# Output powers of S5 batches 5 and 6 made on VectorE ahead of the scan, batch 7 on GpSimd at another place

## The chip, the cores and the metric

The kernel runs on one core of a Trainium2 chip. The metric is the device time of one execution in microseconds (us), lower is better. The engines are TensorE (PE in the profile), its weight load (PEld), VectorE (DVE), ScalarE (ACT), GpSimd (POOL) and the queue of SyncE (SP), which issues most DMAs; ScalarE issues some too (ACTq).

## The reference

Two layers of one trunk, D_MODEL 1024, 256 context and 256 latent tokens. Layer 0 mixes tokens with a bidirectional diagonal state-space layer (S5) and a GLU, layer 1 with a gated DeltaNet; each layer ends with a squared-ReLU MLP. The change lies in S5:

```python
def _s5_direction(u, a_bar, b_bar, c_mat, h0, reverse, need_out):
    bu = jnp.einsum('blgh,gph->lbgp', u.astype(jnp.complex64), b_bar)
    ...
    a = jnp.broadcast_to(a_bar, (bu.shape[0], 1) + a_bar.shape)
    _, h = lax.associative_scan(_linear_recurrence, (a, bu), axis=0)
    final = h[-1]
    ...
    y = jnp.einsum('lbgp,ghp->blgh', h, c_mat).real
```

There are 64 groups of 16 channels with 64 complex states each; the context is scanned first, the latent tokens start from its final state.

## The kernel before, in words

The S5 phase (`s5_phase`) cuts the 64 groups into eight batches of eight, and time into chunks of eight tokens. For each batch b:

- `s5_w` (the W stage): VectorE multiplies powers of the state matrix, which TensorE has spread into a PSUM bank (`ebx`), with the input matrices (`bcB`, loaded by SP). `mul_bc` issues three operations for each half of a direction: a product to a temporary (`wtmp`, in the PSUM bank "scan"), a product to W, and their sum; that is 12 operations of 128x512 a batch.
- `s5_in`: TensorE turns W (`sint`), ScalarE copies it (`Sin`), TensorE multiplies with the input (`xin`), and ScalarE copies the result to X, the per-chunk inputs of the scan.
- `s5_v`: the same products for the output side. The powers are spread into PSUM (`ecx`), copied by ScalarE to `ec`, and multiplied with the output matrices `bcC` (two buffers; `s5_vload` loads the next batch's inside `s5_v`). All eight V are made on GpSimd, in six operations of 128x1024. `s5_v` also lets ScalarE make C0 (C in the rows) from bcC.
- `s5_a8` puts the power for one chunk into the bank "scan". `s5_scan` then walks over the chunks on VectorE: 31 steps for the first half (context), 32 for the second. A step is two `scanm` products and two sums into X (X_83 in the order's rows is the context's half, X_84 the latent's).
- `s5_k`, for pairs p of batches (0 to 3): TensorE makes a strip per batch from V, W and C0, ScalarE copies it and issues four DMAs of it to DRAM (`kd`), SP reads it back in eight DMAs as the Toeplitz tile `Kt` (two buffers), TensorE multiplies (`yl`) and ScalarE copies to `yT`.
- `s5_out(b, 0)` after the first half: ScalarE copies states (`Hs`), TensorE multiplies with V (`yp`), ScalarE applies GELU (`yg`), VectorE turns it (`yT`). `s5_out(b, 1)` does so for the second half. The GLU (weights split into `whi` and `wlo`) and the MLP follow, then the second layer.

No order is written out. Each piece is a `Task` with a priority and the tasks that it comes after; `drive` always takes the next step of the task that a modelled clock lets start first, and records its instructions in that order with their priorities. So a change of one task can move others, and the second layer is planned with a clock whose start is set against that of the first. The early pool (`ce`, with lam, sel, pw and the W tiles) is closed once the W stage and a8 are planned, and the late pool takes its memory, tile by tile, each writer waiting for the readers of what lay there. Nearly all instructions are recorded by one helper, so the profile has them under L268, and they are told apart by tile names.

Of the kernel before, what the change touches and what calls it, by code (L numbers as in the profile page):

```python
# [8 lines left out]
F32 = mybir.dt.float32  # L9
# [306 lines left out]
def drive(clock, tasks, grain=0.25, until=None):  # L316

    live = [t for t in tasks if t.end is None]
    while live and not (until and all(t.end is not None for t in until)):
        best = None  # L320
        for t in live:
            if any(d.end is None for d in t.after) or t.held or (t.gate and t.gate.free == 0):
                continue
            start = max([t.ready] + [d.end for d in t.after])
            start = clock.probe(t.eng, start)[0] if clock.fill and t.eng != "sync" else max(start, clock.t.get(t.eng, 0.0))
            key = (int(start / grain), t.prio)
            if best is None or key < best[0]:
                best = (key, t)
        assert best, "no step can go on"
        t = best[1]  # L330
        clock.step = 0.0
        clock.prio = t.prio
        try:
            r = next(t.gen)
            t.gate = r if isinstance(r, Slots) else None
            t.held = r is HOLD
            if r is HOLD:
                continue
            for o in live:
                o.held = False  # L340
            if not t.gate:
                t.ready = clock.step if r is None else r
        except StopIteration:
            t.end = t.ready = max(t.ready, clock.step)
            live.remove(t)
            for o in live:
                o.held = False
    clock.prio = None
    clock.base = clock.tc.cur_priority = clock.base + 400000
    return live  # L350
# [98 lines left out]
class K:  # L449
# [63 lines left out]
    def ada(self, l, b, pool):  # L513

        nc = self.nc
        acc = self.bank(f"ada{l}{b}", "ada", bufs=1)
        bias = pool.tile([128, 512], F32, name="adab", bufs=1)
        for kt in range(8):
            if kt == 0:
                nc.sync.dma_start(bias, self.I["ada_b"][l, b])  # L520
            while len(self.aw.get((l, b), ())) < 2 * kt + 2:
                yield HOLD
            ws = self.aw[l, b][2 * kt:2 * kt + 2]
            yield ws[1][2]
            for q in range(4):
                nc.tensor.matmul(acc[32 * q:32 * q + 32, :], self.crep[:, kt].rearrange("p a b -> p (a b)"),
                                 ws[q // 2][0][:, q % 2 * 512:q % 2 * 512 + 512], start=kt == 0, stop=False, skip_group_check=True)
            if kt == 6:
                nc.tensor.matmul(acc, self.ident, bias, start=False, stop=False, skip_group_check=True)
            for _, ring, _ in ws:  # L530
                if ring:
                    ring.give()
            yield
        row = pool.tile([128, 512], F32, name="arow", tag="adab", bufs=1)
        nc.scalar.copy(row, acc)
        if b:
            self.arow[l, b] = self.dram.tile([128, 512], F32, name=f"arow{l}{b}")
            nc.sync.dma_start(self.arow[l, b], row)
        yield
        tp = self.bank(f"adat{l}{b}", "aux", bufs=self.naux) if self.naux else self.bank(f"adat{l}{b}")  # L540
        for q in range(4):
            nc.tensor.transpose(tp[:, q * 128:q * 128 + 128], row[:, q * 128:q * 128 + 128], self.ident)
        src = tp.rearrange("p (q v j s r) -> p v j q s r", q=4, v=2, j=2, s=2)
        for v in range(2):
            dst = self.mcol[l][:, 2 * b + v].rearrange("p s (j q) -> p j q s", j=2)
            nc.scalar.copy(dst, src[:, v, :, :, :, 0])
        yield
# [240 lines left out]
    def s5_v(self, b, Vv, eng, late):  # L788

        nc = self.nc  # L790
        yield from self.Cslots.take()
        bc = self.bcC[b]
        ec = self.ec[b]
        self.Vt[b] = Vv
        C0 = self.C0[b] = late.tile([128, 2, 8, 16], F32, name="C0", bufs=NC0)
        nc.scalar.activation(C0, bc[:, 0], AF.Identity, scale=self.nsg)
        for d in range(2):
            dve = eng is nc.vector
            tmp = late.tile([128, 8, 4 if dve else 8, 16], F32, name="vtmp" + "d" * dve, bufs=1)
            self.mul_bc(eng, Vv[:, d], tmp, ec[:, :, :, d], bc[:, :, d], d == 1)  # L800
            if d == 0 and b < 7:
                self.s5_vload(b + 1, late)
            yield

    def s5_k(self, p, late):
# [449 lines left out]
def s5_phase(ctx, k):  # L1255

    nc = k.nc
    with ExitStack() as cs:
# [5 lines left out]
        V57 = [k.long.tile([128, 2, 8, 8, 16], F32, name=f"V{b}") for b in (5, 6)]  # L1264
# [5 lines left out]
        k.nsg = mid.tile([128, 1], F32, name="nsg")  # L1270

        def ecs(b):
            p = k.bank("ecx")[:, 0:256]
            k.expand(p.rearrange("p (k l d g) -> p k l d g", k=2, l=8, d=2), k.pw, b, (2, 3))
            k.ec[b] = mid.tile([128, 2, 8, 2, 8], F32, name="ec", bufs=3)
            nc.scalar.copy(k.ec[b].rearrange("p a b c d -> p (a b c d)"), p)

            yield

        def vgen(b):  # L1280
            Vv = V57[b - 5] if b in (5, 6) else (k.long if b < NV else k.late).tile([128, 2, 8, 8, 16], F32, name=f"V{b}")
            yield from k.s5_v(b, Vv, nc.vector if b in VD else nc.gpsimd, mid)

        def seq(*gens):
            for g in gens:
                yield from g

        T = Task
        VD = ()
        NV = 7  # L1290
        we, ws, ins, V, Kk, outs = [], [], [], {}, {}, []
        k.early = E = k.pool(ce, "early", 1)
# [24 lines left out]
        lds = T(seq(ld, *(k.ada_load(l, b) for l, b in more)), 0, [], "sync")  # L1317
        a0 = T(k.ada(0, 0, mid), 0, [], "tensor")
        a1 = T(seq(*(k.ada(l, b, mid) for l, b in more)), 9, [a0], "tensor")
        xn = T(xg, 1, [], "vector")  # L1320
        u = T(k.s5_u(mid), 2, [a0, xn], "vector")
        for b in range(8):
            we.append(T(k.s5_we(b), 2, we[-1:], "tensor"))
            ws.append(T(k.s5_w(b), 3, ws[-1:] + we[-1:], "vector"))
            ins.append(T(k.s5_in(b), 4, [ws[b], u] + ins[-2:-1], "tensor"))
        a8 = T(k.s5_a8(), 3, [ws[-1]], "vector")
        Ec = []
        for b in range(8):
            Ec.append(T(ecs(b), 1, Ec[-1:] + [V.get(b - 3)], "tensor"))
            if b >= NV:  # L1330
                break
            V[b] = T(vgen(b), 5, [V.get(b - 1 - (b - 1 in VD)), Ec[b]], "gpsimd")
        k.Kslots = Slots(0)
        for p in range(NV // 2):
            Kk[p] = T(k.s5_k(p, mid), 5, [V[2 * p + 1], u, ws[2 * p + 1]], "tensor")
        rest = drive(k.clock, [lds, a0, a1, xn, u, a8] + we + ws + ins + Ec + list(V.values()) + list(Kk.values()), until=ins + Ec + [a8])
        ce.close()
        k.late = k.pool(cs, "late", 1, reuse_waits="tile")
        k.yT = k.late.tile([128, 8, 512], F32, name="yT")
        k.ktp = k.pool(ck, "kt", 1, side="right", reuse_waits="tile")  # L1340
        k.Kslots.free = NKT
        scan = [T(k.s5_scan(0, 31), 0, [], "vector"), T(k.s5_scan(31, 63), 0, [], "vector")]
        scan[0].after += ins
        scan[1].after = [scan[0]]
        for b in range(NV, 8):
            V[b] = T(vgen(b), 5, [V.get(b - 1 if b not in VD and b - 1 not in VD else b - 2), Ec[b]] if b not in VD else [Ec[b]], "vector" if b in VD else "gpsimd")
        for p in range(NV // 2, 4):
            Kk[p] = T(k.s5_k(p, mid), 2, [V[2 * p + 1]], "tensor")
        for b in range(8):
            outs.append(T(k.s5_out(b, 0), 1, [Kk[b // 2], scan[0]] + outs[-1:], "tensor"))  # L1350

        rest = drive(k.clock, rest + scan + [V[b] for b in range(NV, 8)] + [Kk[p] for p in range(NV // 2, 4)] + outs,
                     until=outs + [a1, lds])
# [16 lines left out]
        rest = drive(k.clock, rest + outs + ys[0] + ys[1] + [glu, ld, sp], until=ys[1] + [glu])  # L1370
# [745 lines left out]
def tile_backbone(ctx, tc, *args):  # L2116
# [5 lines left out]
    k.wraw = k.pool(ctx, "wraw", 4, side="right")  # L2122
    c0 = ctx.enter_context(ExitStack())
    xr, cg, rest = s5_phase(c0, k)
    k.stream = Stream(k, nc.vector)
    cp = ctx.enter_context(ExitStack())
# [90 lines left out]
```

## Time and profile before

| | |
|---|---|
| timed runs | 1636.46 us median of 3 (1634.3 to 1636.75) |
| profiled execution | 1630.61 us, span 1628.8 us |
| mean granted clock of TensorE | 0.951 |
| busy: PE, DVE, ACT, POOL | 1467.9, 1105.0, 777.4, 654.3 us |

The span is the stretch of the trace from the first to the last instruction; the profiled execution's own time is 1.81 us more. Busy shares are averages over stages with different limits. In the rows, "[14.74 <-ACT X]" says that the engine stood idle for 14.74 us ahead of this instruction and that ScalarE's write of X ended the wait. A row with x4 has four instructions of one kind in a run.

### The profile page before, as it was taken

The page shows a single profiled execution, that of the slowest core. Times are in us where ns is not written, and L with a number is a line of the kernel's source. Part 1 is how long each engine was busy: PE and PEld are TensorE (multiplying, and loading weights), DVE is VectorE, ACT ScalarE, POOL GpSimd, SP SyncE. Part 2 cuts the span into 40 slices and gives each one's busy share as a digit, 9 for nine tenths or more (in the row PEclk, how much of TensorE's full clock was granted, in tenths as well). Part 3 has the DMA queues.
Part 4 walks back from the last instruction along what each step waited for, and adds up shares of the span by engine and source line. Part 5 has one row for each costly group of instructions (what it writes and reads, how often), then busy time and mean ns, then how long its engine had stood idle before and what let it go on. Part 6 is the DMA issues. An engine that isn't in the chain of part 4 may idle for free.

```text
span 1628.8 us, 31232 instructions
## 1 busy us (share of the span) xinstructions
PE 1467.9 (90%) x12370; PEld 1115.7 (68%) x12370; DVE 1105.0 (68%) x2011; ACT 777.4 (48%) x1637; POOL 654.3 (40%) x510
## 2 busy tenths in 40 slices
PE   6895678989999999997968898989999999989998
PEld 2454456767777777786756676767766665689997
DVE  6977798763343343347998878687869765667666
ACT  3352646543222232216456655656565755554443
POOL 3977033622333233334766543343615400014432
PEclk7997889999999999998989999999998999989999
DMA  9786623463544545331222211111211111536552
GB/s 279 264 290 91 137 98 118 156 211 113 172 147 170 188 158 181 139 106 65 79 77 67 66 54 47 53 47 50 70 39 59 44 57 61 188 127 196 182 192 91
DMA packets 76771, 200.77 MB, mean 123 GB/s; under 512 B 8784, under 2 KB 29008, under 8 KB 76368
## 3 DMA queue, kind: packets, MB, share of 16 engines
q1 hardware_dynamic: 76112, 197.78, 37.1%
q10 hardware_dynamic: 512, 0.98, 0.4%
q8 instruction: 97, 1.59, 0.4%
q14 instruction: 50, 0.41, 0.1%
HBM read 192.71 MB, written 6.03 MB: 122 GB/s over the span
## 4 chain that ended last, share of the span: by engine, by line
PE 62%; DVE 20%; ACT 6%; issue 5%; POOL 4%; DMA 3%; SPq 0%; POOLq 0%; DVEq 0%; ACTq 0%
PE w L268 32%; PE proj L268 8%; PE c L268 6%; DVE cacc L268 3%; PE ada L268 3%; DVE X L268 3%; PE wo L268 2%; POOL wlo L268 2%; DVE wlo L268 1%; DVE U L268 1%; DVE scanm L268 1%; DVE gt L268 1%; PE op L268 1%; PE qs L268 1%; DMA wraw<-in_w_dram 1%
## 5 line engine op out<-in xcount | busy, mean ns | idle before, releaser
L268 ACT CAST whi<-wraw 128x1024 fp32r<-128x1024 f32 x221 | 225.6, 1045 | 259.7 <-PE w L268 140.0
L268 POOL TENSOR_TENSOR wlo<-wraw,whi 128x512 fp32r<-128x512 f32 x129 | 181.7, 1427 | 258.4 <-ACT whi L268 233.6
L268 DVE TENSOR_TENSOR wlo<-wraw,whi 128x1024 fp32r<-128x1024 f32 (+1 forms) x189 | 222.0, 1202 | 79.9 <-ACT whi L268 79.3
L268 PE MATMUL w<-hh,whi 128*128 128x256 f32 (+1 forms) x512 | 170.5, 336 | 0.0
L268 PE MATMUL w<-hl,whi 128*128 128x256 f32 (+1 forms) x512 | 168.9, 331 | 0.0
L268 PE MATMUL w<-hh,wlo 128*128 128x256 f32 (+1 forms) x512 | 168.5, 331 | 0.0
L268 POOL TENSOR_TENSOR sq<-rl 128x512 f32<-128x512 f32 (+1 forms) x64 | 62.5, 977 | 217.1 <-ACT rl L268 213.3
L268 PE MATMUL w<-whi,h1h 128*128 128x512 f32 x384 | 148.8, 395 | 0.0
L268 PE MATMUL w<-whi,h1l 128*128 128x512 f32 x384 | 148.5, 390 | 0.0
L268 PE MATMUL w<-wlo,h1h 128*128 128x512 f32 x384 | 148.4, 389 | 0.0
L268 PE MATMUL proj<-hh,whi 128*128 128x256 f32 (+1 forms) x360 | 130.6, 363 | 10.3 <-ACT pp L268 8.4
L268 DVE TENSOR_TENSOR ma<-w,g 128x512 f32<-128x512 f32 x96 | 65.3, 687 | 103.5 <-PE w L268 103.4
L268 PE MATMUL proj<-hh,wlo 128*128 128x256 f32 (+1 forms) x360 | 125.5, 349 | 1.7 <-POOL wlo L268 1.7
L268 PE MATMUL proj<-hl,whi 128*128 128x256 f32 (+1 forms) x360 | 126.9, 352 | 0.0
L268 DVE SCALAR_TENSOR_TENSOR cacc<-pp,cw,cacc 128x520 f32<-128x520 f32 (+1 forms) x128 | 115.3, 903 | 11.5 <-ACT cacc L268 9.9
L268 POOL TENSOR_TENSOR xr<-xr,ma 128x512 f32<-128x512 f32 x56 | 81.3, 1455 | 95.9 <-DVE ma L268 95.9
L268 PEld LDWEIGHTS w<-hh,whi 128*128 128x128 f32 x512 | 98.0, 192 | 18.1 <-DVE wlo L268 4.2
L268 DVE TENSOR_TENSOR h1l<-sq,h1h 128x512 fp32r<-128x512 f32 (+1 forms) x64 | 35.5, 555 | 106.4 <-POOL sq L268 104.0
L268 PEld LDWEIGHTS w<-hl,whi 128*128 128x128 f32 x512 | 98.2, 192 | 10.5 <-issue 1.9
L268 PEld LDWEIGHTS w<-hh,wlo 128*128 128x128 f32 x512 | 97.9, 192 | 9.8 <-issue 0.8
L268 ACT ACTIVATE v<-c,vsc 64x128 f32<-64x128 f32 x224 | 80.6, 362 | 50.0 <-PE c L268 42.6
L268 POOL TENSOR_TENSOR rstd<-ms,mhalf 128x1 f32<-128x1 f32 (+2 forms) x22 | 17.3, 788 | 191.1 <-DVE ms L268 191.1
(312 smaller groups left out, 3532.2 us busy)
## 6 DMA issues: line engine op xcount, KB each, us to landing
wraw<-in_w_dram SPq DMA_DIRECT2D x128, 512.0 KB, 4.3
adaw<-in_ada_w_dram SPq DMA_DIRECT2D x92, 512.0 KB, 4.8
wraw<-in_w_in_dram SPq DMA_DIRECT2D x48, 512.0 KB, 3.2
wraw<-in_w_glu_dram SPq DMA_DIRECT2D x32, 512.0 KB, 3.3
wraw<-in_w_out_dram SPq DMA_DIRECT2D x16, 512.0 KB, 3.2
Kt<-kd SPq DMA_DIRECT2D x32, 128.0 KB, 4.9
X<-grd SPq DMA_DIRECT2D x32, 128.0 KB, 3.0
V<-in_ada_w_dram SPq DMA_DIRECT2D x4, 512.0 KB, 5.9
```

What stands on the lines that cost most here:

```text
L268: r = f(*args, **kw)
```

## The change

`VD` names the batches whose V is made on VectorE; it was empty and is now 5 and 6. Their powers stay in PSUM (`ecx` in the "hold" banks), their temporary (`vtmpd`) lies in the "scan" bank, and their output matrices come into a tile of their own, `bcCd`, with one buffer, loaded by SP inside `s5_v`. These tasks come after the last W task, and a8 comes after V[6]. V of batch 7 stays on GpSimd, comes after V[4], and is now the first tile of the late pool. The load of the ada bias (`adab`) gets the highest priority.

```diff
@@ ada
             if kt == 0:
+                prio, self.clock.prio = self.clock.prio, None if self.clock.prio is None else 0
                 nc.sync.dma_start(bias, self.I["ada_b"][l, b])
+                self.clock.prio = prio
@@ s5_v
+        dve = eng is nc.vector
         yield from self.Cslots.take()
+        if dve:
+            self.bcC[b] = self.early.tile([128, 2, 2, 8, 16], F32, name="bcCd", bufs=1)
+            nc.sync.dma_start(self.bcC[b], self.I["bc"][b, 1])
...
         for d in range(2):
-            dve = eng is nc.vector
-            tmp = late.tile([128, 8, 4 if dve else 8, 16], F32, name="vtmp" + "d" * dve, bufs=1)
+            tmp = (self.bank("vtmpd", "scan", bufs=1).rearrange("p (g t c) -> p g t c", g=8, t=4) if dve else
+                   late.tile([128, 8, 8, 16], F32, name="vtmp", bufs=1))
             self.mul_bc(eng, Vv[:, d], tmp, ec[:, :, :, d], bc[:, :, d], d == 1)
-            if d == 0 and b < 7:
-                self.s5_vload(b + 1, late)
+            if d == 0 and b < 7 and not dve:
+                self.s5_vload({4: 7}.get(b, b + 1), late)
+            if d and dve:
+                self.Hslots.give()
@@ s5_phase
         def ecs(b):
+            if b in VD:
+                yield from k.Hslots.take()
+                p = k.ec[b] = k.bank("ecx", "hold", bufs=2)[:, 0:256].rearrange("p (k l d g) -> p k l d g", k=2, l=8, d=2)
+                k.expand(p, k.pw, b, (2, 3))
+                yield
+                return
...
-        VD = ()
+        VD = (5, 6)
...
-        a8 = T(k.s5_a8(), 3, [ws[-1]], "vector")
...
-            V[b] = T(vgen(b), 5, [V.get(b - 1 - (b - 1 in VD)), Ec[b]], "gpsimd")
+            V[b] = T(vgen(b), 5, [V.get(b - 1), Ec[b]], "vector" if b in VD else "gpsimd")
+        a8 = T(k.s5_a8(), 3, [V[6]], "vector")
...
         k.late = k.pool(cs, "late", 1, reuse_waits="tile")
+        k.V7 = k.late.tile([128, 2, 8, 8, 16], F32, name="V7")
...
-            V[b] = T(vgen(b), 5, [V.get(b - 1 if b not in VD and b - 1 not in VD else b - 2), Ec[b]] if b not in VD else [Ec[b]], "vector" if b in VD else "gpsimd")
+            V[b] = T(vgen(b), 1, [V[4], Ec[b]], "gpsimd")
```

On VectorE, at the end of the W stage, the order now reads as follows (V_80 is batch 5's V, V_81 batch 6's; each group of three stands four times for a batch).

```order
L268 TENSOR_TENSOR W<-W,wtmp 128x8x64
L268 TENSOR_TENSOR vtmpd<-ecx,bcCd 128x512
L268 TENSOR_TENSOR V_80<-ecx,bcCd 128x8x64
L268 TENSOR_TENSOR V_80<-V_80,vtmpd 128x8x64
...
L268 TENSOR_TENSOR V_81<-V_81,vtmpd 128x8x64
L268 COPY scan<-pw 128x64 x2
L268 TENSOR_SCALAR scan<-pw 128x64
L268 COPY scan<-pw 128x64
```

Before, the first COPY of a8 followed on the W row; 24 operations have come between. On GpSimd, the end of V reads so in the kernel before (V_1361 is batch 7's):

```order
L268 TENSOR_TENSOR V_736<-V_736,vtmp 128x1024
L268 TENSOR_TENSOR V_81<-ec,bcC 128x1024 x2
...
L268 TENSOR_TENSOR V_1361<-ec,bcC 128x1024 x2
...
L268 TENSOR_TENSOR V_1361<-V_1361,vtmp 128x1024
L268 TENSOR_TENSOR wlo<-wraw,whi 128x512 x6
```

and so with the change (V_749 is batch 4's, V_1373 batch 7's):

```order
L268 TENSOR_TENSOR V_749<-V_749,vtmp 128x1024
L268 TENSOR_TENSOR vtmp<-ec,bcC 128x1024
L268 TENSOR_TENSOR V_1373<-ec,bcC 128x1024 x2
L268 TENSOR_TENSOR V_1373<-V_1373,vtmp 128x1024
L268 TENSOR_TENSOR vtmp<-ec,bcC 128x1024
L268 TENSOR_TENSOR V_1373<-V_1373,vtmp 128x1024
L268 TENSOR_TENSOR wlo<-wraw,whi 128x512 x6
```

The rows of batches 5 and 6 are gone, and five operations of batch 7 stand behind its first vtmp. On ScalarE, the stretch from the second pair's strips to the first yg reads so before (kd_1678 is pair 2's, kd_1832 pair 3's):

```order
L268 DMA kd_1507<-strip 16x960 x4
L268 COPY strip<-strip 128x480 x2
L268 DMA kd_1678<-strip 16x960 x3
L268 COPY yT<-yl 128x512
L268 DMA kd_1678<-strip 16x960
L268 COPY strip<-strip 128x480
L268 COPY yT<-yl 128x512
L268 COPY strip<-strip 128x480
L268 DMA kd_1832<-strip 16x960 x4
L268 COPY yT<-yl 128x512 x4
L268 COPY Hs<-X_83 64x2x128 x8
```

and so with the change (kd_1664 is pair 3's, kd_1860 pair 2's):

```order
L268 DMA kd_1664<-strip 16x960 x4
L268 COPY yT<-yl 128x512 x2
L268 COPY strip<-strip 128x480
L268 COPY yT<-yl 128x512 x2
L268 COPY strip<-strip 128x480
L268 DMA kd_1860<-strip 16x960 x2
L268 COPY yT<-yl 128x512
L268 DMA kd_1860<-strip 16x960 x2
L268 COPY yT<-yl 128x512
L268 COPY mcol_97<-adat_1849 128x8x2 x2
L268 COPY arow<-ada_1865 128x512
L268 COPY Hs<-X_83 64x2x128 x8
```

Pair 3 now comes ahead of pair 2; the yT copy between the kd issues of pair 2 is that of batch 6, and the copy arow has come ahead of Hs.

## Rows read from the trace of the kernel before

**Rows 1.** The page: its first line, and a line of its DMA issues (KB each, median us to landing).

```profile
span 1628.8 us, 31232 instructions
...
bcC<-in_bc_dram SPq DMA_DIRECT2D x8, 256.0 KB, 5.1
```

**Rows 2.** Stretches: busy us of each engine (instructions), PEclk, DMA share, GB/s.

```profile
115.00:180.00 65.00, 37.27 (x1036) 31.33 (x1032) 47.96 (x130) 18.35 (x40) 34.34 (x16) 0.77 0.71 115
...
371.00:600.00 229.00, 229.00 (x1084) 175.43 (x1084) 86.50 (x96) 68.45 (x92) 74.88 (x56) 1.00 0.46 157
...
775.00:1450.00 675.00, 613.80 (x6426) 452.38 (x6427) 521.92 (x1069) 398.57 (x1009) 264.92 (x214) 0.95 0.20 67
```

**Rows 3.** The chain that ended last, 80 to 330: start us, us, what.

```profile
127.24 2.54 DMA bcC<-in_bc_dram
...
149.77 2.42 DVE X L268
181.35 0.65 ACT Hs L268
```

**Rows 4.** Timeline of VectorE: start us, us, engine, operation, tiles [idle before <-releaser].

```profile
98.11 0.70 DVE L268 TENSOR_TENSOR wtmp<-ebx,bcB 128x512 f32<-128x512 f32 x1 [1.54 <-DMA bcB<-in_bc_dram]
...
114.52 0.49 DVE L268 COPY scan<-pw 128x64 f32<-128x64 f32 x2
...
115.31 0.23 DVE L268 COPY scan<-pw 128x64 f32<-128x64 f32 x1
...
130.86 3.30 DVE L268 TENSOR_TENSOR X<-X,scanm 128x128 f32<-128x128 f32 x2 [14.74 <-ACT X L268]
...
148.08 4.10 DVE L268 TENSOR_TENSOR X<-X,scanm 128x128 f32<-128x128 f32 x2
...
152.62 0.61 DVE L268 TENSOR_TENSOR X<-X,scanm 128x128 f32<-128x128 f32 x2
...
230.36 0.68 DVE L268 TENSOR_TENSOR wlo<-wraw,whi 128x512 fp32r<-128x512 f32 x1
```

**Rows 5.** Timeline of GpSimd, 116 to 152.

```profile
122.70 2.40 POOL L268 TENSOR_TENSOR V<-V,vtmp 128x1024 f32<-128x1024 f32 x1
...
129.95 4.07 POOL L268 TENSOR_TENSOR V<-ec,bcC 128x1024 f32<-128x1024 f32 x2 [0.29 <-DMA bcC<-in_bc_dram]
...
149.67 2.36 POOL L268 TENSOR_TENSOR V<-V,vtmp 128x1024 f32<-128x1024 f32 x1
```

**Rows 6.** Timeline of ScalarE and its DMA queue (ACTq), 126 to 194.

```profile
129.81 0.51 ACT L268 ACTIVATE C<-bcC,nsg 128x256 f32<-128x256 f32 x1 [2.53 <-DMA bcC<-in_bc_dram]
...
131.70 3.13 ACTq L268 DMA_DIRECT2D kd<-strip  x4
...
163.53 2.60 ACTq L268 DMA_DIRECT2D kd<-strip  x4
...
179.42 5.20 ACT L268 COPY Hs<-X 64x256 f32<-64x256 f32 x8 [5.20 <-DVE X L268]
...
186.69 0.38 ACT L268 ACTIVATE yg<-yp 128x256 f32<-128x256 f32 x1
...
193.24 0.59 ACT L268 COPY arow<-ada 128x512 f32<-128x512 f32 x1
```

**Rows 7.** Timeline of SP's DMA queue, three windows of it.

```profile
136.62 17.95 SPq L268 DMA_DIRECT2D Kt<-kd  x16
...
158.22 6.23 SPq L268 DMA_DIRECT2D Kt<-kd  x8
...
170.18 5.45 SPq L268 DMA_DIRECT2D Kt<-kd  x8
```

**Rows 8.** Timeline of TensorE, 160 to 235.

```profile
169.75 3.85 PE L268 MATMUL yl<-Kt,U 128*32 128x128 f32 x64 [4.15 <-DMA kd<-strip]
...
181.35 2.36 PE L268 MATMUL yl<-Kt,U 128*32 128x128 f32 x40 [6.92 <-ACT Hs L268]
...
231.10 0.80 PE L268 MATMUL glu<-wlo,yh 128*128 128x512 f32 x1 [8.20 <-DVE wlo L268]
```

More of the change, by code (lines that the diff above doesn't have):

```diff
@@ L1280, in vgen @@
         def vgen(b):
-            Vv = V57[b - 5] if b in (5, 6) else (k.long if b < NV else k.late).tile([128, 2, 8, 8, 16], F32, name=f"V{b}")
+            Vv = V57[b - 5] if b in (5, 6) else k.V7 if b == 7 else k.long.tile([128, 2, 8, 8, 16], F32, name=f"V{b}")
             yield from k.s5_v(b, Vv, nc.vector if b in VD else nc.gpsimd, mid)
@@ L1325, in s5_phase @@
             ins.append(T(k.s5_in(b), 4, [ws[b], u] + ins[-2:-1], "tensor"))
-        a8 = T(k.s5_a8(), 3, [ws[-1]], "vector")
         Ec = []
         for b in range(8):
-            Ec.append(T(ecs(b), 1, Ec[-1:] + [V.get(b - 3)], "tensor"))
+            Ec.append(T(ecs(b), 1, Ec[-1:] + [ws[-1] if b in VD else V.get(b - 3 if b < 7 else 4)], "tensor"))
             if b >= NV:
                 break
-            V[b] = T(vgen(b), 5, [V.get(b - 1 - (b - 1 in VD)), Ec[b]], "gpsimd")
+            V[b] = T(vgen(b), 5, [V.get(b - 1), Ec[b]], "vector" if b in VD else "gpsimd")
+        a8 = T(k.s5_a8(), 3, [V[6]], "vector")
         k.Kslots = Slots(0)
@@ L1335, in s5_phase @@
             Kk[p] = T(k.s5_k(p, mid), 5, [V[2 * p + 1], u, ws[2 * p + 1]], "tensor")
-        rest = drive(k.clock, [lds, a0, a1, xn, u, a8] + we + ws + ins + Ec + list(V.values()) + list(Kk.values()), until=ins + Ec + [a8])
+        rest = drive(k.clock, [lds, a0, a1, xn, u, a8] + we + ws + ins + Ec + list(V.values()) + list(Kk.values()), until=ins + Ec + [a8, V[5], V[6]])
         ce.close()
         k.late = k.pool(cs, "late", 1, reuse_waits="tile")
+        k.V7 = k.late.tile([128, 2, 8, 8, 16], F32, name="V7")
         k.yT = k.late.tile([128, 8, 512], F32, name="yT")
```

## The prediction

> **What bounds the kernel now.** I began with the page: the profiled execution has a span of 1628.8 us [rows 1], and its own time is 1630.61, 1.81 more. The three timed runs have their median at 1636.46, so 5.85 us are added when a sum made against the profile is compared with runs. The stretches come next [rows 2]. From 371 to 600 TensorE is busy for the whole 229 us, so whatever reaches that stretch earlier or later shifts the end by as much. From 115 to 180, where the change lies, TensorE is busy for 37.27 of 65 us: something else sets the pace. The chain that ended last [rows 3] says what: the load of bcC at 127.24, then VectorE's X, which is the scan, until 152, then ScalarE's copies Hs.
>
> The timeline of VectorE [rows 4] shows the same from the inside. The 24 operations of the W stage for batches 6 and 7 fill 98.11 to 114.5, so 8.2 us a batch; the first had waited 1.54 for bcB. The four a8 operations end at 115.54. Then VectorE stands still for 14.74 until the last X copy, which ScalarE held behind a C0 activation that waited 2.53 for bcC [rows 6]. That bcC was issued only when GpSimd gave its buffer free [rows 3]. From 130.86 two X operations take 3.3 to 4.1 us as long as GpSimd works, and 0.61 after it stops at 152.03 [rows 4, 5]. Five of the 31 steps of the first half are done at 152.2 and the other 26 at 179.42, where the Hs copies start [rows 6]: 1.047 us a step. After that ScalarE makes the outputs, the first yg at 186.69, and on VectorE the wlo that TensorE waits 8.20 for stands behind scan steps [rows 4, 8].
>
> One more chain runs beside this. A pair's strip goes to DRAM (kd) and comes back as Kt, and TensorE's yl needs all eight Kt transfers. From a pair's first Kt issue to its yl pass 11.5 us (158.22 to 169.75) and 11.2 (170.18 to 181.35) [rows 7, 8]. From the end of the last kd issue to the first Kt pass 1.8 (134.83 to 136.62) and 4.05 (166.13 to 170.18) [rows 6, 7]. The yl of 181.35 feeds a yT copy that stands ahead of the first yg: 5.3 us from yl to yg.
>
> **The change, part by part.** *V5 and V6 on VectorE.* Each is 12 operations of 128x512 of the W stage's three kinds with a tmp in PSUM; the trace has no such row for V, the W rows are the nearest, so 8.2 us each. I take the 1.54 wait as gone, since that bcB now stands ahead of adaw loads that it had stood behind (bounds 0 and 1.54). The W stage then ends at 113.0 and V5 at 121.2. The bcCd of batch 6 has one buffer, is issued when V5's last multiply is done (about 120.5), and needs 2.54 [rows 3] to 5.1 (the median of the eight bcC loads) [rows 1]; with 2.54 V6 waits 1.9, with 5.1 it waits 4.4. I take 2.54, the row that stood alone on the queues, as this one will. V6 ends at 131.3, a8 at 132.3. The X copies of batch 7 no longer stand behind a bcC wait and are done by then, so the old 14.74 has been filled with work: the scan starts 1.4 later than before.
>
> *V5 and V6 off GpSimd, V7 at its new place.* Twelve operations go. V7's first vtmp can run early, but its first write lies in memory that a8 reads, so five operations (2.0, 2.0, 2.4, 2.0, 2.4 by [rows 5]) run from 132.3 to 143.1 under the scan. Each holds one X operation, as the rows of 130.86 to 152 show, so two and a half steps are done at 143.1 and the other 28.5 take 29.8: the first half ends at 172.9 instead of 179.42, 6.5 earlier.
>
> Here a rule is weighed. The rows say that the X pair pays 4.10 and GpSimd nothing: its V<-V,vtmp is 2.40 ahead of the scan and 2.36 under it [rows 4, 5]. The Trainium skill ("SBUF — State Buffer", section "Who interferes with whom") states that a VectorE operation with two SBUF inputs and a GpSimd operation that reads SBUF exclude each other for a whole instruction, whoever started first. By that rule V7's operations would wait for X operations too, some 0.3 us each (half of 0.61), V7 would end 1.5 later and so would all that hangs on it, 1638.4 in place of the forecast's 1636.9; by the rows it is nothing, and the sum goes by the rows.
>
> *The K chain in its new order: pairs 0, 1, 3, 2.* V7's strip (40 small matmuls and a copy) I bound by the pace of yl, 64 in 3.85, at 2.4 us; kd of pair 3 starts at 145.5, its four issues take 2.6 [rows 6], to 148.1, and with 4.05 the first Kt is issued at 152.2. It used to be pair 2's at 158.22. Its yl comes 11.2 later, at 163.4. Now the order costs something: on ScalarE the last two kd of pair 2 stand behind the yT copy of batch 6, which needs that yl (half of 3.85, and 0.6 for the copy): 165.9. Two issues of 0.65 bring 167.2, the way to the first Kt is 1.8 to 4.05 (I take the middle, 2.9, since only two transfers are left to land), so pair 2's first Kt is issued at 170.1 and its yl starts at 181.3. Before, the last yl started at 181.35. In the old order kd of the last pair lay beside the Kt of the pair ahead; in the new one it lies behind it, and what GpSimd's earlier end gave is spent there. The first yg stays at 186.7.
>
> *The rest.* The copy arow of 0.59 moves from between yg operations [rows 6] to ahead of the Hs copies, where ScalarE has time: 0.6 gained. On VectorE one more scan step stands ahead of the wlo that TensorE waits for at 231.10 [rows 8], since the transposes moved further ahead in the scan than that wlo did: 1.05 lost. The adab issue and one wraw issue change place on SP's queue beside work that lasts longer: nothing, and at most their own half microsecond.
>
> *Sum:* 0.0 from the last yl, -0.6, +1.05: +0.4 us, so 1631.0 for the profiled execution and 1636.9 on the scale of the median. Its own range goes by the bounds of kd's way: 1.8 takes 1.1 away and 4.05 adds 1.2, so 1635.8 to 1638.1 with the other waits as taken.
>
> **The rivals.** *The scan's gain arrives.* If the kd transfers are not late, since queues are emptier and V7's strip is quick, the 6.5 us of the scan reach the outputs: -6.5 - 0.6 + 1.05 = -6.0, so 1630.5. For it speaks that the chain that ended last names DVE X and not Kt at 150 [rows 3]; against it that the last yl started after the scan's half had ended already before (181.35 against 179.42).
>
> *The K chain comes late* (the other side). V6's bcCd takes 5.1 instead of 2.54 (+2.5), the wait for bcB stays (+1.5), and kd's way is 4.05 (+1.2): all hang on one line from V6 over V7 to pair 2's Kt, so they add up: +5.2 - 0.6 + 1.05 = +5.7, 1642.2. It decides from the point where pair 2's first Kt is issued after 173.0 (170.1 + 2.9): then the loss is over 3.3. For it speaks that three of four links have a row with the longer time; against it that those rows were taken with other transfers in flight.
>
> *The later phase is planned anew.* The planner starts the second layer from a clock that moved, and between 800 and 1440 neighbours change place on all engines. TensorE is idle there for 675.00 - 613.80 = 61.2 us [rows 2]. An estimate of a tenth of it either way is 6.1 us: 1630.8 or 1643.0. Nothing in the trace says which sign.
>
> *It does nothing* falls together with the forecast, as the sum shows.
>
> **How the numbers follow.** About 0.2% (3.3 us) is what a measurement of this kernel can tell from no change. I give the forecast 0.42 (of it 0.07 faster, 0.30 same, 0.05 slower, for smaller amounts of the other cases), the scan's gain 0.19 (0.17 faster, 0.02 same), the late K chain 0.20 (0.17 slower, 0.03 same), the new plan 0.19 (0.08, 0.03, 0.08). That makes 0.32 faster, 0.38 same, 0.30 slower. The predicted time is the forecast's, 1636.9. The range takes in the scan's gain with 1.5 us to spare and reaches past both slower cases: 1629 to 1643.5.
>
> **What would show it.** In the profile after: 24 operations vtmpd and V on VectorE of 0.7 each from about 113, with a wait for bcCd of about 2 in the middle; a8's end near 132 and no wait of X behind it; X pairs of about 4 until 143 and 0.61 after; the Hs copies free to start near 173; the first Kt of the last pair near 170 and its yl near 181, with ScalarE idle in between; the first yg near 186.7. If yg comes before 184, the kd and Kt times were taken too long, and the forecast fails to the fast side; if the last Kt is issued after 173, to the slow side. If the outputs are where I put them and the time still differs by more than 3 us, the second layer's new order did it, and the stretch 775 to 1450 shows it in TensorE's idle time.

## The result, and the profile after

| | before | after |
|---|---|---|
| median of the runs, us | 1635.38 (1634.15 to 1636.75, 4 runs) | 1659.42 (1657.06 to 1663.16, 4 runs) |
| profiled execution: span, us | 1628.8 | 1661.4 |
| profiled execution: its own time, us | 1630.61 | 1663.16 |
| first yg copy on ScalarE | 186.69 | 194.16 |
| a VectorE wlo in the middle of the first layer's MLP | 428.69 | 438.21 |
| a VectorE wlo near the end of the second layer | 1554.05 | 1586.60 |

The ratio is 1.0149, with a 95% interval of [1.0127, 1.0171]: 24 us slower, against a forecast of 1636.9 and a range that ended at 1643.5. Each of the last three rows of the table is the start of one and the same instruction in the two traces. They show two losses: 7.5 us at the first yg and 9.5 by the first layer's MLP, and another 23 between the MLP and the end of the second layer (1148.39 from one wlo to the other, where it had been 1125.36). The profiled execution of before is 5 us below the median of its runs and that of after 4 above its own. On the scale of the medians the second loss is 24.0 - 9.5 = 14.5 us.

The stretches of the changed kernel, to be read beside [rows 2] (busy us of PE, PEld, DVE, ACT and POOL with their instruction counts, granted clock, DMA share, GB/s):

```profile
115.00:180.00 65.00, 34.37 (x976) 27.05 (x976) 55.26 (x157) 14.13 (x31) 10.75 (x5) 0.79 0.66 124
...
371.00:600.00 229.00, 229.00 (x1070) 172.91 (x1068) 85.73 (x96) 64.54 (x88) 74.07 (x55) 0.99 0.47 159
...
775.00:1450.00 675.00, 607.71 (x6356) 444.51 (x6355) 513.24 (x1040) 390.89 (x990) 264.16 (x213) 0.94 0.19 62
```

GpSimd does what the change says, 34.34 us of work down to 10.75 in the first stretch, and VectorE takes it over. The MLP is TensorE alone, as before, and hands on whatever delay reaches it. From 775 to 1450, in the second layer, TensorE stands idle for 675.00 - 607.71 = 67.3 us instead of 61.2, at a granted clock of 0.94 and 0.95 (mostly the upper of its two levels). These two windows do not hold the same instructions. From one wlo of the table to the other they do, first before, then after:

```profile
428.69:1554.05 1125.36, 1051.78 (x8712) 810.49 (x8713) 745.96 (x1336) 556.58 (x1246) 427.75 (x346) 0.97 0.31 103
438.21:1586.60 1148.39, 1066.12 (x8712) 819.78 (x8713) 750.00 (x1336) 558.72 (x1246) 426.03 (x346) 0.95 0.31 101
```

Of the 23.0 us, 8.7 are idle time of TensorE (82.3 instead of 73.6). In the other 14.3 it is busy longer with the same 8712 instructions, at a granted clock of 0.95 instead of 0.97.

VectorE's timeline of the changed kernel, beside [rows 4]:

```profile
120.35 0.69 DVE L268 TENSOR_TENSOR V<-V,vtmpd 128x512 f32<-128x512 f32 x1
127.91 0.70 DVE L268 TENSOR_TENSOR vtmpd<-ecx,bcCd 128x512 f32<-128x512 f32 x1 [6.87 <-DMA bcCd<-in_bc_dram]
...
136.09 0.49 DVE L268 COPY scan<-pw 128x64 f32<-128x64 f32 x2
...
137.60 3.84 DVE L268 TENSOR_TENSOR X<-X,scanm 128x128 f32<-128x128 f32 x2
...
141.87 4.00 DVE L268 TENSOR_TENSOR X<-X,scanm 128x128 f32<-128x128 f32 x2
...
146.31 2.31 DVE L268 TENSOR_TENSOR X<-X,scanm 128x128 f32<-128x128 f32 x2
...
149.05 0.61 DVE L268 TENSOR_TENSOR X<-X,scanm 128x128 f32<-128x128 f32 x2
...
194.58 0.45 DVE L268 STREAM_TRANSPOSE yT<-yg 128x256 f32<-128x256 f32 x1 [12.39 <-ACT yg L268]
```

The same transpose in the kernel before:

```profile
187.11 0.45 DVE L268 STREAM_TRANSPOSE yT<-yg 128x256 f32<-128x256 f32 x1 [2.81 <-ACT yg L268]
```

V5 ends at 121.04 (120.35 + 0.69). V6 then waits 6.87 for its matrices. The scan starts at 137.20 and is slow until GpSimd's V7 ends, then runs at the old pace. From three steps done at 148.65 and 28 more of 1.047 its first half ends at 178.0, 1.4 earlier than before. The scan is not late. The loss shows in the wait of 12.39 us at 194.58, where it had been 2.81: VectorE stands at a transpose that waits for ScalarE's first yg, and the scan's second half stands behind it.

SP's DMA queue shows why V6 waited:

```profile
105.46 12.37 SPq L268 DMA_DIRECT2D adaw<-in_ada_w_dram  x8
121.52 0.80 SPq L268 DMA_DIRECT2D wraw<-in_w_glu_dram  x2
122.38 0.42 SPq L268 DMA_DIRECT2D bcCd<-in_bc_dram  x1
...
162.71 3.50 SPq L268 DMA_DIRECT2D Kt<-kd  x5
176.88 0.34 SPq L268 DMA_DIRECT2D adab<-in_ada_b_dram  x1
177.40 5.10 SPq L268 DMA_DIRECT2D Kt<-kd  x8
```

and in the kernel before:

```profile
175.74 0.54 SPq L268 DMA_DIRECT2D adab<-in_ada_b_dram  x1
```

The buffer for batch 6's bcCd was free at about 120.3, but two wraw loads stood ahead of the load and could themselves be issued only at 121.52. It went at 122.38 and V6 started 5.5 later. At the other end pair 2's Kt (the x8) began at 177.40. The bias load adab stood ahead of it, but SP still waited 0.2 us for kd behind adab, so adab cost it nothing here.

ScalarE and its DMA queue, beside [rows 6]:

```profile
151.21 2.37 ACTq L268 DMA_DIRECT2D kd<-strip  x4
...
159.92 0.56 ACT L268 COPY strip<-strip 128x480 f32<-128x480 f32 x1 [5.16 <-DMA kd<-strip]
...
163.43 2.09 ACTq L268 DMA_DIRECT2D kd<-strip  x2
174.35 0.58 ACT L268 COPY yT<-yl 128x512 f32<-128x512 f32 x1 [11.57 <-PE yl L268]
174.36 0.78 ACTq L268 DMA_DIRECT2D kd<-strip  x2
...
184.03 0.59 ACT L268 COPY arow<-ada 128x512 f32<-128x512 f32 x1 [6.89 <-PE ada L268]
184.51 5.07 ACT L268 COPY Hs<-X 64x256 f32<-64x256 f32 x8
191.24 0.59 ACT L268 COPY yT<-yl 128x512 f32<-128x512 f32 x1 [1.66 <-PE yl L268]
...
194.16 0.38 ACT L268 ACTIVATE yg<-yp 128x256 f32<-128x256 f32 x1 [1.04 <-PE yp L268]
```

Pair 3's kd goes at 151.21, pair 2's first half at 163.43, and its second half waits 11 us more behind a yT copy that needs pair 3's products. Then arow, which stands ahead of the eight Hs copies, waits 6.89 for TensorE. The Hs copies start at 184.51, though the scan's first half has been done since 178. TensorE's rows, beside [rows 8], close the ring:

```profile
148.20 0.60 PE L268 MATMUL strip<-V,W 128*32 128x112 f32 x8 [9.63 <-POOL V L268]
...
172.15 3.86 PE L268 MATMUL yl<-Kt,U 128*32 128x128 f32 x64 [9.70 <-DMA Kt<-kd]
...
175.94 0.90 PE L268 MATMUL adat<-consts,arow 128*128 128x128 f32 x3
...
180.17 2.02 PE L268 MATMUL ada<-adab,consts 128*128 128x512 f32 x2 [3.32 <-DMA adab<-in_ada_b_dram]
...
189.25 2.79 PE L268 MATMUL yl<-Kt,U 128*32 128x128 f32 x48 [5.32 <-ACT Hs L268]
```

The ada product that arow waits for had to wait 3.32 for adab. SP issued adab at 176.88, after 8.2 us of waiting for TensorE's adat (arow and adab share one buffer), and adat stands behind pair 3's yl. In the kernel before adab went at 175.74, hardly earlier; what is new is that the Hs copies stand behind arow. So the chain is: V6 late, V7 late, pair 3's strip late, its yl at 172.15, the second half of pair 2's kd, its Kt, and beside it adat, adab, ada, arow, Hs and yg.

### The profile page after: what moved, and what is told of

Read it like the earlier page. It is cut to its first block, busy times and chain, and to the rows that moved or that the text cites. A ratio compares the mean times of both kernels' runs of the same rounds, so it can differ in the third digit from the quotient of the medians.

```text
span 1661.4 us, 31225 instructions
## 1 busy us (share of the span) xinstructions
PE 1482.7 (89%) x12370; PEld 1126.0 (68%) x12370; DVE 1114.8 (67%) x2035; ACT 779.8 (47%) x1635; POOL 631.2 (38%) x498
## 4 chain that ended last, share of the span: by engine, by line
PE 63%; DVE 16%; ACT 6%; DMA 6%; issue 5%; POOL 4%; SPq 1%; ACTq 0%; POOLq 0%; DVEq 0%
PE w L268 31%; PE proj L268 8%; PE c L268 7%; DVE cacc L268 3%; PE ada L268 3%; PE wo L268 2%; DVE vc L268 2%; POOL V L268 1%; DVE wlo L268 1%; DMA adaw<-in_ada_w_dram 1%; DVE gt L268 1%; PE qs L268 1%; ACT Hs L268 1%; PE op L268 1%; DVE X L268 1%
## 5 line engine op out<-in xcount | busy, mean ns | idle before, releaser
L268 PE MATMUL proj<-hh,whi 128*128 128x256 f32 (+1 forms) x360 | 134.8, 374 | 11.0 <-ACT pp L268 10.7
L268 DVE SCALAR_TENSOR_TENSOR cacc<-pp,cw,cacc 128x520 f32<-128x520 f32 (+1 forms) x128 | 111.4, 872 | 13.6 <-ACT cacc L268 12.3
```

The source lines that it names most:

```text
L268: r = f(*args, **kw)
```

## The experiments

Two theories stood against each other from the start: that S5 alone loses the 24 us, or that S5 loses some 9.5 and the second layer, whose instructions the change does not touch, loses the rest by standing in another order. Both kernels write the second layer's instructions down in the same sequence. The framework's scheduler then places each where its own timeline has it ready, and that timeline had moved: in the two stored orders of e1 and e2, 4719 of TensorE's 6680 instructions from the second layer's start stand at different places.

The table holds all runs. "Start of MLP wlo" and "second layer" come from one profiled execution each: the start of the wlo at 428.69 of before, and the distance to the wlo at 1554.05. The first of these columns is rough: e6, e9 and e10 have the same first layer in the same order and lie at 426.41, 428.65 and 423.56. The kernel before, timed in the same sets of runs, had medians of 1637.04 (19 runs, 1630.22 to 1646.16), 1636.81 (25 runs) and 1637.01 (17 runs). The ratios are not exactly those of these medians: e1's is 1.0094, where the medians give 1.0076.

| kernel | second layer's order | median | ratio, 95% interval | MLP wlo | second layer |
|---|---|---|---|---|---|
| before | before's | 1637 | 1 | 428.69 | 1125.36 |
| after | after's | 1659.42 | 1.0149 [1.0127, 1.0171] | 438.21 | 1148.39 |
| e1: after | before's | 1649.56 | 1.0094 [1.0064, 1.0125] | 437.96 | 1135.53 |
| e2: before | after's | 1649.42 | 1.0092 [1.0061, 1.0122] | 427.31 | 1146.12 |
| e3: after, bcC of batch 6 early | before's | 1636.66 | 1.0011 [0.9987, 1.0035] | 425.75 | 1134.37 |
| e4: after, K2 ahead | before's | 1637.30 | 1.0017 [1.0000, 1.0033] | 426.79 | 1132.16 |
| e5: after, arow behind Hs | before's | 1644.77 | 1.0049 [1.0024, 1.0074] | 435.74 | 1126.01 |
| e6: e3 and e4 | before's | 1633.19 | 0.9985 [0.9960, 1.0009] | 426.41 | 1134.30 |
| e7: e3, pairs in order | before's | 1646.77 | 1.0061 [1.0038, 1.0084] | 441.12 | 1136.22 |
| e8: before, plan +0.3 us | its own | 1680.17 | 1.0267 [1.0222, 1.0312] | 425.98 | 1170.45 |
| e9: e6 again | before's | 1636.36 | 0.9990 [0.9969, 1.0011] | 428.65 | 1135.82 |
| e10: e3 and e4 | its own | 1625.46 | 0.9934 [0.9909, 0.9960] | 423.56 | 1123.32 |
| e11: before, plan -0.3 us | its own | 1655.49 | 1.0116 [1.0087, 1.0145] | 427.91 | 1152.86 |

**e1 and e2: the order of the second layer exchanged.** Nothing is added or taken out; edges that only order fix each engine's sequence from the second layer's start to that of the other kernel:

```
+    for e, ks in ORDER.items():          # stored places, engine by engine
+        for a, b in zip(ks, ks[1:]):
+            tc.add_manual_dep(rec[b][1], rec[a][1].name, DependencyInfo(NoSync, DATA))
```

> The changed kernel, with one thing fixed: from the start of the second layer to the end, each engine's instructions stand in the order that they have in the kernel before (order-only edges, no operation added or removed). Theory of two losses: the first layer's S5 loses about 9.5 us (the first yg copy at 194.2 against 186.7, the MLP 9.2 to 9.5 behind throughout), and the rest of the 24 us comes from the second layer's instructions standing in another order than before. Then this kernel takes 1635.4 + 9.5 = about 1645 us, and behind the MLP its lag stays at 9 to 10 us. Rival, that the second layer's loss has another source than its order (the granted clock, transfers that fall elsewhere): 1655 to 1660 us, and the lag grows in the second layer as in the changed kernel.

> The kernel before, with its second layer's instructions fixed to the order that they have in the changed kernel; S5 of the first layer stays as it was. Theory of two losses: 1635.4 + 14.5 = about 1650 us, with no lag up to the end of the MLP at 775 us. Rival, that the order alone costs nothing and the second layer suffers from something that the changed S5 does to it: 1634 to 1638 us.

The stretch 775 to 1450 in e1 and then in e2 (columns as above):

```profile
775.00:1450.00 675.00, 612.21 (x6390) 448.93 (x6389) 520.66 (x1055) 393.83 (x998) 263.95 (x213) 0.95 0.20 67
```

```profile
775.00:1450.00 675.00, 610.23 (x6328) 444.50 (x6328) 514.65 (x1045) 389.23 (x985) 258.62 (x208) 0.94 0.20 66
```

e1 costs 12.5 us over before and e2 costs 12.4 (1649.56 and 1649.42 against 1637.04). Together that is 24.9, where the change lost 24.0; by the ratios it is some 15 each, with intervals of 10 to 20, so the sum holds to within several us. In both, TensorE, VectorE and ScalarE run the second layer in the other kernel's sequence. Each half of the change's loss can be had without the other, so the two-loss theory holds and both rivals fall. In e2 the MLP is where it was, and 12 us are lost in a layer that no line of the change touches. The size in e1 was off: 12.5 instead of 9.5. The MLP lags 9.3 as expected, so some 3 us more go in its second layer. In that layer e1's TensorE was granted 0.93 from 1000 to 1200 where before had 0.97 with the same order. The last section sets this beside the other runs.

**e3: V6's wait taken away.** The second layer keeps before's order here and in e4 to e7 and e9, so that only S5 is compared.

```
-            self.bcC[b] = self.early.tile(..., name="bcCd", bufs=1)
-            nc.sync.dma_start(self.bcC[b], self.I["bc"][b, 1])
+            for x, name in ((5, "bcCd"), (6, "bcB")) if b == 5 else ():
+                self.bcC[x] = self.early.tile(..., name=name, bufs=1 if x == 5 else 2)
+                nc.sync.dma_start(self.bcC[x], self.I["bc"][x, 1])      # with priority 0
```

> As the run of the changed kernel with the second layer in the order of before, and one part of the change undone in addition: the output matrices of batch 6 do not wait for the single buffer bcCd, but are loaded into the ring bcB together with those of batch 5, ahead of V5. Theory, that the 6.87 us wait of V6 for its matrices is handed through the wrapped-state task, batch 7 on GpSimd and the K chain of pair 3 to the scan's first output: V6 starts about 6.9 us earlier, the last Hs copies and the first yg up to 6 us earlier, so about 1639 to 1641 us against 1645 of the run without it. Rival, that the K chain of pair 2 and the row of the adaptive norm set the end whatever V6 does: V6 starts 6.9 earlier and the time is within 2 us of the run without it.

VectorE's first operation of V6, and below it ScalarE's rows around the first yg:

```profile
120.45 0.70 DVE L269 TENSOR_TENSOR vtmpd<-ecx,bcB 128x512 f32<-128x512 f32 x1 [0.94 <-PE ecx L269]
```

```profile
168.42 0.59 ACT L269 COPY yT<-yl 128x512 f32<-128x512 f32 x1 [9.69 <-PE yl L269]
168.43 0.78 ACTq L269 DMA_DIRECT2D kd<-strip  x2
...
170.69 5.17 ACT L269 COPY Hs<-X 64x256 f32<-64x256 f32 x8
176.83 0.58 ACT L269 COPY arow<-ada 128x512 f32<-128x512 f32 x1 [0.96 <-PE ada L269]
...
178.72 0.38 ACT L269 ACTIVATE yg<-yp 128x256 f32<-128x256 f32 x1
```

The wait is gone (0.94, and for another tile), V6 starts 6.0 earlier than in e1 (126.49; 2.4 of it because V5 ended earlier in this execution), and the first yg comes at 178.72 instead of 191.69 in e1. The time falls by 12.9 us against e1, where the theory had 4 to 6 (1639 to 1641 against 1645). One reason is in the rows: with V6 early the scheduler also put arow behind the Hs copies, so two links of the chain went at once. The second half of pair 2's kd still stands behind yT, at 168.43. The run therefore shows that V6's wait and what the schedule hung on it make up the S5 loss, not how much the wait is worth alone.

**e4: the queue positions alone.** V6 still waits 5.62 here.

```
+        k.behind(M["yT", 6][:1], M["kd", 2])          # ScalarE: copy of batch 6 behind kd of pair 2
+        k.behind(M["adab", (0, 2)], M["Kt", 2])       # SP: bias load behind Kt of pair 2
+        k.behind(M["arow", (0, 2)], M["Hs", (0, 1)])  # ScalarE: row behind the eight Hs copies
```

> As the run of the changed kernel with the second layer in the order of before, with order-only edges in the K chain: ACT issues the last two descriptor copies kd of pair 2 before the output copy of batch 6, SP issues Kt of pair 2 before the load of the adaptive norm's bias, and ACT makes the norm's row behind the first eight state copies Hs, not ahead of them. The stall of V6 for its matrices stays. Theory, that queue positions alone cost most of the S5 loss (a kd issue 11 us behind its partner, Kt of pair 2 at 177.4, Hs held 6.9 us by the row): Kt of pair 2 starts at about 171, its yl products at about 183, the first yg at about 188.4 and the time is about 1639 to 1640 us. Rival, that V6's stall is what matters: within 2 us of the run without the edges, about 1645 us.

```profile
161.83 3.79 ACTq L269 DMA_DIRECT2D kd<-strip  x4
171.25 0.59 ACT L269 COPY yT<-yl 128x512 f32<-128x512 f32 x1 [11.06 <-PE yl L269]
...
177.24 5.15 ACT L269 COPY Hs<-X 64x256 f32<-64x256 f32 x8 [3.54 <-DVE X L269]
183.88 0.58 ACT L269 COPY yT<-yl 128x512 f32<-128x512 f32 x1 [1.49 <-PE yl L269]
...
186.02 0.38 ACT L269 ACTIVATE yg<-yp 128x256 f32<-128x256 f32 x1 [0.25 <-PE yp L269]
```

All four kd issues of pair 2 stand together, the Hs copies wait for the scan and for nothing else, and yl and yg follow within a microsecond or two. The first yg is at 186.02, level with before, and the time falls by 12.3 us. So the late V6 by itself costs little: e6 and e9, which take its wait away as well, are 4.1 and 0.9 us faster than this run. It costs because pair 2's transfers and arow stand behind what it delays. The edge on adab was not run alone; by the rows of the changed kernel adab did not hold Kt up.

**e5: one of the three edges, arow behind Hs.**

> As the run of the changed kernel with the second layer in the order of before, with one order-only edge: the row of the adaptive norm is copied behind the first eight state copies Hs on ACT instead of ahead of them. Pair 2's last descriptor copies and the bias load stay where the change put them. Theory, that the row in front of Hs is one of two parts of the S5 loss: Hs starts when the scan's first half ends, at about 177 instead of 181.6, the first yg at 187 instead of 191.7, and the time falls by 4 to 5 us against 1649.6. Rival A, that pair 2's late products set the end alone: within 1.5 us of 1649.6. Rival B, that the row was all of what the three edges of the earlier run recovered: 1637 to 1639.

```profile
174.70 5.16 ACT L269 COPY Hs<-X 64x256 f32<-64x256 f32 x8 [1.64 <-DVE X L269]
179.89 0.59 ACT L269 COPY arow<-ada 128x512 f32<-128x512 f32 x1
187.77 0.59 ACT L269 COPY yT<-yl 128x512 f32<-128x512 f32 x1 [7.29 <-PE yl L269]
...
190.20 0.38 ACT L269 ACTIVATE yg<-yp 128x256 f32<-128x256 f32 x1 [0.55 <-PE yp L269]
```

The median fell by 4.8, as expected, but the trace says otherwise. Hs moved by 7 us and the first yg by 1.5 only, since yT now waits 7.29 for pair 2's products. At the MLP 2.2 us are won, less than that column can tell. This kernel's runs spread over 15 us (1638.30 to 1653.44), the profile is of the fastest of them, and the ratio's interval overlaps that of e1. So the rows make arow the small part and pair 2's way the large one, nearer to rival A than the median suggests; how much arow is worth in the time stays open.

**e6 and e9: e3 and e4 together.**

> Batch 6's output matrices loaded early, and the three order-only edges (pair 2's descriptor copies ahead of the output copy of batch 6, the bias load behind Kt of pair 2, the row behind Hs), both with the second layer in the order of before. Each alone came out at 1637, level with the kernel before, with a first layer that ends 2 to 3 us ahead of it. Theory, that the two shorten the same chain and what is left waits for the scan's second half on DVE (the GLU's wlo behind it): the first layer ends 2 to 4 us ahead of before and the time is 1633 to 1637. Rival, that they are separate losses and add: the first layer ends 10 us or more ahead of before, 1624 to 1628.

> The kernel of the run with early matrices and the three order-only edges, second layer in the order of before, measured again in more rounds, since its ratio of 0.9985 [0.9960, 1.0009] left open whether it beats the kernel before. Theory, that with the K chain out of the way the change is worth a little: 1632 to 1635 us, a ratio of 0.997 to 0.9995. Rival, that it is level: 0.9995 to 1.001.

The first yg comes at 177.69 in e6 and 182.67 in e9, 9 and 4 us before that of the kernel before, but the MLP's wlo is only 2.3 us ahead of before in one profile and level with it in the other (426.41 and 428.65 against 428.69; e2, e8 and e11, whose S5 is before's, lie at 425.98 to 427.91). So the gains of e3 and e4 do not add, as the theory said. With before's order in the second layer the change is level with before: 0.9985 and 0.9990, both intervals across 1. e9 does not tell its theory from its rival: its ratio is inside the theory's range and its median outside.

**e7: the pairs back in the order 0, 1, 2, 3, with the matrices early.**

```
-            Kk[p] = T(k.s5_k(p, mid), 2, [V[2 * p + 1]], "tensor")
+            Kk[p] = T(k.s5_k(p, mid), 6, [V[2 * p + 1]], "tensor")
+        k.behind(M["kd", 3][:1], M["kd", 2])        # and six more edges of this kind
```

> Batch 6's output matrices loaded early, and the K chain's pairs planned and queued in the order 0, 1, 2, 3, as before the change, instead of 0, 1, 3, 2 (pair 3's priority made lower than pair 2's, and order-only edges that keep copies, transposes, the bias load and the row behind them); second layer in the order of before. Theory, that the swapped pair order is part of the S5 loss and no gain of its own: Kt of pair 2 lands before 165, the last half of the products waits for pair 3 instead, and the time is within 2 us of the run with early matrices alone, 1635 to 1639. Rival, that finishing pair 2 first frees the output path: 3 us or more faster than that run.

```profile
167.50 0.59 ACT L269 COPY yT<-yl 128x512 f32<-128x512 f32 x1 [1.02 <-PE yl L269]
...
170.21 2.20 ACTq L269 DMA_DIRECT2D kd<-strip  x4
...
187.83 0.59 ACT L269 COPY yT<-yl 128x512 f32<-128x512 f32 x1 [7.54 <-PE yl L269]
...
192.45 0.59 ACT L269 COPY arow<-ada 128x512 f32<-128x512 f32 x1 [2.33 <-PE ada L269]
...
194.34 0.38 ACT L269 ACTIVATE yg<-yp 128x256 f32<-128x256 f32 x1
```

A miss on both sides: 10.1 us slower than e3. In this plan the four yT copies of pairs 0 and 1 stand ahead of pair 3's strip copies and kd on ScalarE, so this kd went at 170.21 (at 145.04 in e3), and arow again stood ahead of yg. It tells little about the pair order. It does show the same mechanism a second time: a kd behind yT copies that wait for products, and yg 15.6 us later than in e3.

**e8 and e11: the second layer's plan moved by 0.3 us in the kernel before.**

```
-GDN0 = 803.4465179647354
+GDN0 = 803.4465179647354 + 0.3        # e11: - 0.3
```

> The kernel before, with the time at which the planner starts the second layer's plan moved by 0.3 us (a number in the plan alone, no operation added, S5 untouched). The second layer's instructions then stand in another order in very many places. Theory, that any such reordering of the second layer costs or gains several us and that the 12 us it cost the changed kernel are a draw of this kind: a time that differs from the kernel before by 3 us or more to either side, with no lag before 775 us. Rival, that only the order that follows from the changed S5 is costly: within 2 us of the kernel before.

> The kernel before, with the start of the second layer's plan moved by 0.3 us to the other side. The run with +0.3 took 1680 us. Theory, that any move draws another order: not 1637 but anywhere from 1630 to 1690, with no lag before 775 us. Rival, that a later start is what costs and an earlier one does not: 1633 to 1640 us.

e8's stretch 775 to 1450:

```profile
775.00:1450.00 675.00, 589.34 (x6227) 429.81 (x6227) 493.39 (x1009) 374.87 (x959) 252.72 (x204) 0.93 0.18 57
```

43 us lost by +0.3 and 18.5 by -0.3, with S5 and the MLP untouched (425.98 and 427.91). In this window TensorE is idle for 85.7 us in e8 instead of 61.2. From wlo to wlo its second layer takes 45.1 us longer, of which 31.2 are idle time and 13.9 longer busy. The rival, that only a later start costs, falls. The number of instructions that moved does not tell the price: by operation, tile and shape 4786 of TensorE's last 6680 in e8, 4710 in e11, 4308 in the changed kernel.

**e10: e3 and e4, the second layer in whatever order comes out.**

> The same first layer (early matrices, three order-only edges), but without the fixed order of the second layer: its instructions stand as they come out for this kernel, in a third order. Theory, that the second layer's order is a draw that has nothing to do with the merit of the first layer's change: up to 775 us as the run with the fixed order, and then a time that differs from it by 3 us or more to either side, up to +40. Rival, that the costly order of the changed kernel was caused by its late K chain: 1632 to 1636 us, as with the fixed order.

VectorE's first transpose, and then the stretch 775 to 1450:

```profile
177.54 0.45 DVE L268 STREAM_TRANSPOSE yT<-yg 128x256 f32<-128x256 f32 x1 [3.07 <-ACT yg L268]
```

```profile
775.00:1450.00 675.00, 614.58 (x6475) 454.70 (x6474) 517.77 (x1070) 404.10 (x1014) 262.94 (x212) 0.95 0.21 68
```

1625.46 us, 0.66% faster than the kernel before and the fastest median of all. The 12.39 at the transpose is 3.07. Against e6 and e9 only the second layer's order differs, and that is worth 7.7 and 10.9 us by the medians and 11.0 and 12.5 from one wlo to the other. So the gain is real for this program, but it is luck in the order: with before's order the moved output powers are level by e6 and e9. Whether this order is better than before's own is not shown: in the single profiles its second layer is 2.0 us shorter than before's.

## Why the prediction was wrong

*W stage, V5, V6's own length, V7 under the scan: right.* The W stage ended at 112.8 (forecast 113.0), V5 at 121.04 (121.2), and the 24 operations took 0.7 each. V7 took 10.9 us under the scan (137.24 to 148.14), and its three X pairs 3.84, 4.00 and 2.31: as forecast from [rows 4, 5]. The rule weighed there, of the Trainium skill ("SBUF — State Buffer", section "Who interferes with whom"), holds on VectorE's side alone in these rows. GpSimd's five operations sum to 10.8 us and the stage lasted 10.9, so the 1.5 us that GpSimd should wait by the rule are not in this trace.

*The step that failed first: "the bcCd of batch 6 is issued when V5's last multiply is done (about 120.5), and needs 2.54".* It was issued at 122.38 and landed 5.5 later, so the wait was 6.87 and not 1.9 (4.57, 5.62 and 4.31 in e1, e4 and e5). I had priced the transfer from the fastest row and had not looked at what stands ahead of it on SP's queue. e3 and e6 show that an early load removes it.

*The step that made it dear: "two issues of 0.65 bring 167.2, the way to the first Kt is 1.8 to 4.05".* The two issues ended at 175.1 and pair 2's first Kt came at 177.40. It came 7.3 us after the 170.1 of the forecast, and of these the stall of V6 made up 5.0 (6.87 - 1.9). The other large part is the way of pair 3's kd: 6.3 from the end of its issues (151.21 + 2.37) to the ScalarE copy that waits for it to land (159.92), where I took 4.05. The smaller terms cancel: the strip took 0.7 and the way from Kt to yl 1.0 more than I had (my 11.2 was read off a yl that [rows 8] put down to Hs, not to Kt), the issues and the last way, 2.3 and inside its bounds, 1.7 less. I did name this rival with its decision point, "issued after 173.0", and it happened; I priced it at 5.7 and it cost 9.3 to 10.7 at the MLP. I had also given it and the new plan as cases that exclude each other, and both came.

*arow, "0.6 gained": the sign was wrong.* Ahead of the Hs copies it waited 6.89 for TensorE's ada, which waited for adab, which waited for an adat behind pair 3's yl. I had moved the copy and not what feeds it. Put back alone, it moved the first yg by 1.5 us and the median by 4.8 (e5); together with pair 2's issues and the bias load, nearly all of the S5 loss (e4: 12.3 us of 12.5).

*"1.05 lost" on VectorE: too small.* The transposes that moved ahead in the scan wait for yg in program order, so a late yg stops the scan's second half: 12.39 us in one row, 2.81 before. This is the way by which the K chain's delay reached the GLU.

*The second layer, "an estimate of a tenth of it either way is 6.1 us": a term of the right kind, wrongly sized.* e2 puts it at 12.4 us for the order alone, some 14 in the changed kernel. The tenth came from TensorE's idle time in one schedule. The kernels with an order of their own run from 12 us faster than before (e10, with its first layer) to 43 slower (e8), far beyond this term, and a range for such a change has to be wider to the slow side. The test that the prediction set for this, "775 to 1450 shows it in TensorE's idle time", pointed the right way (67.3 and 85.7 against 61.2) but shows a part only: idle time is 8.7 of the 23.0 us from wlo to wlo, and in 14.3 TensorE is busy longer with the same instructions, which the prediction had no term for.

## What to carry to other kernels

Where a scheduler orders later code from a simulated clock, an edit upstream changes that code too. Fix the later order to that of the kernel before and time the edit alone, and time the later orders by themselves; here this split 24 us into 12 and 12 and found a version 0.66% faster than the kernel before. When a step is moved on an in-order queue, look up what feeds each instruction that now stands ahead of others, DMA issues included. A copy of 0.59 us held eight others up for 6.89 because its input was late, and a load of 256 KB with two others ahead of it on its queue stopped VectorE for 6.87.

## What the runs showed that I had not expected

The load of bcCd took 5.5 us from its issue to its use (4.6 in e1, e4 and e5); a bcC of the same 256 KB had taken 2.54 in [rows 3]. Two wraw loads of 512 KB had been issued right ahead of it at 121.52, and eight adaw loads between 105.46 and 117.83. I had expected it to travel alone. That these loads made it slower is likely, but no run takes them away.

The second layer's time differs by 47 us over the orders tried (1123.32 to 1170.45 between the two wlo), and TensorE's granted clock differs with it: over that stretch 0.97 in before and e10, 0.96 in e2, 0.95 in the changed kernel, e8 and e11.

The kernels with before's order fixed add to this. In e5 the second layer took 1126.01, as long as in before (1125.36), so the fixed order as such need not cost anything. In e1, e3, e4, e6, e7 and e9 it took 1132.16 to 1136.22. The granted clock from 1000 to 1200 goes with that: 0.97 in before and e5, 0.93 to 0.96 in the other six. So the few microseconds more in most of these kernels come with a lower clock in that stretch, at the same order of the work. What lowers it, and how much of the loss in the costly orders is the clock's, is not shown. These few microseconds stay below the spread of before's own runs (1630.22 to 1646.16).
